# Second layer's attention scores issued together and later, first layer's output projection summed in three parts

## The chip, the cores and the metric

The program runs on one core of one Trainium2 chip. The metric is the device time of one execution in microseconds (us). The kernel before has a median of 2377.14 us over three runs (2376.62 to 2378.21).

## The reference

A trunk of two layers over 256 tokens of 2048 features, in float32. Cut to what matters here:

```python
h = x
for i in range(2):
    hn = rms_norm(h, attn_norm[i])
    mix = windowed_gqa_sink(hn, ...) if i == 0 else diff_attention(hn, ...)   # each ends in  o @ w_o
    h = h + mix
    h = h + swiglu(rms_norm(h, ffn_norm[i]), w_ffn_in[i], w_ffn_out[i])
    gate = sigmoid(rms_norm(h, ple_gate_norm[i]) @ ple_w_gate[i])
    h = h + rms_norm(p[i] @ ple_w_proj[i], ple_post_norm[i]) * gate

# diff_attention, per head (8 heads, two score maps c = 0, 1 each)
probs_c = softmax(q_c @ k_c.T * scale - slope * dist)
o = (probs_0 - lam * probs_1) @ v
```

Layer 0 has 32 query heads in 16 pairs, and each pair gives 128 of the 2048 columns of `o`, so the projection `o @ w_o` sums over 16 blocks of 128 rows of `w_o`.

## The kernel before

**Weights.** All weights stream from HBM as float32 in blocks of 4 x 128 rows by 512 columns (`load_block`, on SP's queue). `split_block` turns two blocks of 128 rows at a time into a high and a low float32r half: ACT casts the high half (L138, tile `ws`), DVE subtracts for the low one (L139). Four `ws` tiles exist, and the split runs up to four ahead (`feed.ahead`). Each product x*w is three matmuls (high x low, low x high, high x high), so one block of 128 rows costs six matmuls of 128x512 (two token halves `m`, three products) at L176, tile `mm`.

**Groups.** A `Group` is one strip of 512 output columns times `n` row blocks: it takes two of the four `mm` PSUM tiles, runs `n` times six matmuls, and calls `done(ps)`. Before row block `k` it calls `flow.until(len(xs) > k)`: if the activation tile `xs[k]` has not been issued yet, all pending side work is issued at once until it has.

**Side work.** Attention, norms and transposes are small pieces that wait in the heap of `Flow`. `flow.later(delay, fn)` puts a piece in; every weight matmul moves the clock of `Flow` on by `MM` = 0.23 and runs one step of the piece that is due, up to its next `yield`. So a `yield` after each small matmul puts one weight matmul between any two of them. The order on PE is exactly the order of issue; ACT, DVE and POOL are ordered by the tile scheduler, which knows their dependences.

**First layer.** `AttentionA`: 16 pairs of heads, each with scores (L410, 128x512), softmax (`exps`, tile `e`), eight transposes of `e` (`keys_first`, L441, tile `wT`), twelve matmuls with the values (`weigh`, L546, 128x256), and a split into `os[j]` (L206 on ACT and L207 on DVE, tile `xt`). `project(w, os, norm)` is the output projection: in two halves of 8 row blocks, four strips each, so that the first half needs only `os[0]` to `os[7]`. Each group's `done` adds its two PSUM tiles to the residual `h` on DVE (`add_to_h`, L298), and in the second half also starts the next norm of that strip (`norm.add`: squares on ACT at L242, then after a delay of 3.0 eight transposes at L269 and their splits at L210 and L211).

**Second layer.** `AttentionB`: four strips of 512 columns, each with a group for the queries, one for the keys and one for the values, of 16 row blocks each; a strip holds two heads. `turn_side` transposes a head's queries or keys (four matmuls at L402, tile `qk`, split at L210 on ACT and L211 on DVE) and, for the keys, queues the two score maps with delays 4.5 and 6.5. `scores` (L410, here 128x256, six matmuls per map) is followed by `exps` and, after the second map, by the mix of the two maps (`r2l`, a scaling on POOL at L610, DVE at L612), then transposes (L441), values (`weigh`, L635) and the transposes of the result (L658). The second layer's projection uses the same `project`.

The program emits, at the end, `groups = attn_a.groups() + project(...) + FeedForward(0) + attn.groups() + project(...) + FeedForward(1)` and runs them one after the other.

Of the kernel before, what the change touches and what calls it, by code (L numbers as in the profile page):

```python
# [18 lines left out]
P = 128  # L19
# [66 lines left out]
def encoder(ctx: ExitStack, tc: tile.TileContext, x, p, attn_norm, ffn_norm, a_w_qkv, a_q_norm,  # L86
# [189 lines left out]
    class Slots:  # L276
# [5 lines left out]
        def __len__(self):  # L282
            n = 0
            while n in self.got:
                n += 1
            return n
# [118 lines left out]

    def scores(ps, q, k):

        for m in range(NM):
            for i, (a, b) in enumerate(((0, 1), (1, 0), (0, 0))):
                nc.tensor.matmul(ps[m], q[:, a, mslice(m)], k[:, b], start=(i == 0), stop=(i == 2))  # L410
                yield

# [146 lines left out]
    class AttentionB:  # L559
# [18 lines left out]
        def turn_side(self, hd, which, toks, b):  # L578
            s = self.hd.setdefault(hd, {"e": {}})
            t = self.ap.tile([P, 2, 2, T], F32R, name=f"qk{which}", tag=f"qk{which}", bufs=2)  # L580
            yield from to_pairs(t, toks, b * T, (gq_b, gk_b)[which])
            s[which] = t
            if which == 1:
                for c in range(2):
                    flow.later(4.5 + 2.0 * c, lambda c=c: self.scores(hd, c))

# [11 lines left out]
        def scores(self, hd, c):  # L598
# [3 lines left out]
            pss = [ps[:, m, :] for m in range(NM)]  # L602
            yield from scores(pss, s[0][:, c], s[1][:, c])
            s["e"][c] = exps(pss, self.dist, 2.0 ** (-8.0 * (hd + 1) / B_H), self.ap)
# [68 lines left out]

    def project(w, os, norm):

        def done(half, s):
            def add(ps):
                add_to_h(ps, s)
                if half == 1:
                    norm.add(s, 3.0)  # L680
            return add
        n = KT // 2

        class Half:
            def __len__(self):
                return max(0, len(os) - n)

            def __getitem__(self, k):
                return os[n + k]
        return [Group(w, half * n * P, n, s, (os, Half())[half], done(half, s))  # L690
                for half in range(2) for s in range(NS)]

# [120 lines left out]
    norm = Norm(C_FFN)  # L813
    groups = attn_a.groups() + project(a_w_o[0], attn_a.os, norm)
    norm_b = Norm(C_ATTN + KT)
    groups += FeedForward(0, norm).groups(norm_b)
    attn = AttentionB(norm_b)
    norm = Norm(C_FFN + KT)
    groups += attn.groups() + project(b_w_o[0], attn.os, norm)
    groups += FeedForward(1, norm).groups(None)  # L820
# [87 lines left out]
```

## Time and profile before

| what | value |
|---|---|
| median of 3 runs | 2377.14 us (2376.62 to 2378.21) |
| the profiled execution's own time | 2379.22 us |
| its span, first to last instruction | 2377.4 us |
| PE busy | 2347.2 us, 99% of the span |
| DVE busy | 1352.4 us, 57% |
| ACT busy | 1121.4 us, 47% |
| mean granted clock of TensorE | 0.997 of full speed |
| share of PE in the chain that ended last | 87% (L176 alone 84%) |

PE is the matmul side of TensorE, PEld its weight loads. The time of a PE row runs to the modelled end of its last matmul; successive matmuls overlap, so the distance from one start to the next is what a matmul costs in a stream. "Idle before" is the time in which an engine did nothing just before the instruction, with the engine that released it.

### The profile page before, as it was taken

What the parts mean: (1) busy time and instruction counts of PE and PEld (TensorE: products, weight loads), DVE (VectorE), ACT (ScalarE), POOL (GpSimd) and SP (SyncE); (2) the same over time, 40 slices, a digit from 0 to 9 for tenths busy, and PEclk for the clock granted to TensorE, in tenths of its full rate; (3) what the DMA queues carried; (4) which work ended last, traced back from release to release, by engine and by line L of the source; (5) the groups of instructions that cost most, each with busy time, mean ns of one, the idle gap of its engine ahead of it and who ended that gap; (6) DMA issues with size and microseconds to landing.
All of it is one profiled execution on the core that took longest, in us unless ns stands there. A gap on an engine that the chain in (4) does not pass through costs nothing.

```text
span 2377.4 us, 28287 instructions
## 1 busy us (share of the span) xinstructions
PE 2347.2 (99%) x10757; PEld 1928.4 (81%) x10757; DVE 1352.4 (57%) x1604; ACT 1121.4 (47%) x1557; POOL 141.4 (6%) x311
## 2 busy tenths in 40 slices
PE   8999999999999999999999999999999999999999
PEld 6877788888888888888878888888888888888887
DVE  5777555555555454566567667655545554455564
ACT  5555454434434434455555554544444434444453
POOL 1342000000000000000110120000000000000000
PEclk9999999999999999999999999999999999999999
DMA  6433455555555555555544545555555555555554
GB/s 236 158 108 106 137 182 191 195 192 189 192 185 190 195 191 191 185 179 193 181 160 162 175 160 179 190 185 185 195 186 195 194 193 183 192 195 195 177 196 141
DMA packets 121569, 428.71 MB, mean 180 GB/s; under 512 B 13552, under 2 KB 16728, under 8 KB 121176
## 3 DMA queue, kind: packets, MB, share of 16 engines
q1 hardware_dynamic: 121432, 426.89, 51.8%
q8 instruction: 84, 1.38, 0.2%
q14 instruction: 53, 0.43, 0.1%
HBM read 424.74 MB, written 2.10 MB: 180 GB/s over the span
## 4 chain that ended last, share of the span: by engine, by line
PE 87%; DVE 1%; ACT 1%; issue 0%; POOL 0%; DVEq 0%; POOLq 0%; ACTq 0%
PE mm L176 84%; PE at L751 1%; PE at L269 1%; PE at L410 1%; PE at L635 1%; DVE ws L139 0%; ACT e L427 0%; PE at L402 0%; DVE e L612 0%; ACT v L210 0%; PE at L441 0%; ACT ws L138 0%; PE at L658 0%; DVE qk L211 0%; POOL e L610 0%
## 5 line engine op out<-in xcount | busy, mean ns | idle before, releaser
L176 PE MATMUL mm<-ws,xt 128*128 128x512 f32 x9600 | 2315.6, 396 | 6.1 <-ACT xt L206 3.9
L176 PEld LDWEIGHTS mm<-ws,xt 128*128 128x128 f32 x9600 | 1792.1, 188 | 404.9 <-ACT xt L206 4.9
L139 DVE TENSOR_TENSOR ws<-raw,ws 128x1024 fp32r<-128x1024 f32 x800 | 978.0, 1224 | 874.2 <-ACT ws L138 873.5
L138 ACT CAST ws<-raw 128x1024 fp32r<-128x1024 f32 x800 | 840.8, 1052 | 1026.8 <-PE mm L176 957.2
L217 POOL TENSOR_SCALAR rs_v<-ssum 128x2 f32<-128x2 f32 x8 | 1.5, 193 | 1707.5 <-DVE ssum L246 1707.5
L298 DVE TENSOR_TENSOR h<-mm,h 128x512 f32<-128x512 f32 x96 | 62.2, 682 | 2.3 <-PE mm L176 2.2
L210 ACT ACTIVATE xt<-at,gains 128x256 fp32r<-128x256 f32 x96 | 44.1, 474 | 32.9 <-DVE xt L211 24.2
L269 PE MATMUL at<-ident,h 128*128 128x128 f32 x192 | 52.4, 287 | 6.2 <-DMA h<-in_x_dram 6.2
L427 ACT ACTIVATE e<-e,nm 128x257 f32<-128x257 f32 (+1 forms) x96 | 48.0, 503 | 21.1 <-DVE nm L424 20.7
L206 ACT CAST xt<-at 128x256 fp32r<-128x256 f32 x108 | 37.9, 372 | 39.9 <-DVE xt L207 31.8
L211 DVE SCALAR_TENSOR_TENSOR xt<-at,gains,xt 128x256 fp32r<-128x256 f32 x96 | 44.7, 480 | 17.8 <-ACT xt L210 17.8
L207 DVE TENSOR_TENSOR xt<-at,xt 128x256 fp32r<-128x256 f32 x108 | 43.3, 418 | 14.0 <-ACT xt L206 14.0
L219 POOL TENSOR_TENSOR rs_y<-rs_v,halves 128x2 f32<-128x2 f32 (+2 forms) x29 | 49.0, 1691 | 2.4
L751 PE MATMUL at<-ident,hid 128*128 128x128 f32 x176 | 47.8, 272 | 0.0
L546 PE MATMUL at<-wT,vp 128*128 128x256 f32 x192 | 45.7, 297 | 1.3 <-DVE wT L207 1.0
L421 DVE SCALAR_TENSOR_TENSOR e<-dist,at 128x256 f32<-128x256 f32 x96 | 36.4, 413 | 10.2 <-PE at L410 9.8
L441 PE MATMUL at<-ident,e 128*128 128x128 f32 x160 | 40.6, 272 | 0.7 <-DVE e L421 0.7
L410 PE MATMUL at<-kd,qT 128*128 128x512 f32 x96 | 36.1, 400 | 3.2 <-DVE wT L207 2.5
L732 ACT ACTIVATE silu<-mm,rinv 128x512 f32<-128x512 f32 x44 | 29.9, 688 | 19.7 <-PE mm L176 19.7
L526 POOL TENSOR_SCALAR e<-e,rd 128x256 f32<-128x256 f32 x64 | 33.0, 532 | 60.4 <-DVE rd L430 60.0
L546 PEld LDWEIGHTS at<-wT,vp 128*128 128x128 f32 x192 | 33.9, 204 | 2.9 <-ACT e L427 1.1
L269 PEld LDWEIGHTS at<-ident,h 128*128 128x128 f32 x192 | 27.7, 147 | 9.4 <-DMA h<-in_x_dram 7.1
(97 smaller groups left out, 671.7 us busy)
## 6 DMA issues: line engine op xcount, KB each, us to landing
raw<-in_w_ffn_in_dram SPq DMA_DIRECT2D x352, 512.0 KB
raw<-in_w_ffn_out_dram SPq DMA_DIRECT2D x176, 512.0 KB
raw<-in_b_w_qkv_dram SPq DMA_DIRECT2D x96, 512.0 KB
raw<-in_ple_w_gate_dram SPq DMA_DIRECT2D x64, 512.0 KB
raw<-in_a_w_qkv_dram SPq DMA_DIRECT2D x40, 512.0 KB
raw<-in_a_w_o_dram SPq DMA_DIRECT2D x32, 512.0 KB
raw<-in_b_w_o_dram SPq DMA_DIRECT2D x32, 512.0 KB
raw<-in_ple_w_proj_dram SPq DMA_DIRECT2D x16, 256.0 KB
```

Source lines behind the costliest of these rows:

```text
L138: nc.scalar.copy(out=ws[:, 0], in_=src)
L139: nc.vector.tensor_tensor(out=ws[:, 1], in0=src, in1=ws[:, 0].bitcast(F32), op=ALU.subtract)
L176: nc.tensor.matmul(ps[m], x[:, a, mslice(m)], w, start=(k == 0 and i == 0), stop=(k == self.n - 1 and i == 2))
L210: nc.scalar.activation(out=hi, in_=src, func=AF.Copy, scale=scale)
L211: nc.vector.scalar_tensor_tensor(out=lo, in0=src, scalar=scale, in1=hi.bitcast(F32), op0=ALU.mult, op1=ALU.subtract)
L219: nc.gpsimd.tensor_tensor(out=y, in0=v, in1=halves[:, :n], op=ALU.pow)
L269: nc.tensor.transpose(ps[:, j, mslice(m)], h[:, m, (k + j) * P:(k + j + 1) * P], ident)
L298: nc.vector.tensor_tensor(out=hs, in0=ps[m], in1=hs, op=ALU.add)
L410: nc.tensor.matmul(ps[m], q[:, a, mslice(m)], k[:, b], start=(i == 0), stop=(i == 2))
L427: nc.scalar.activation(out=sc[:, m, :], in_=sc[:, m, :], func=AF.Exp, bias=nm[:, m:m + 1], accum_out=den[:, m:m + 1])
L546: nc.tensor.matmul(ps, v[:, a, c0:c0 + P], wT[:, b, kh, :], start=(n == 0), stop=(n == 11))
L751: nc.tensor.transpose(ps[:, j, mslice(m)], hid[m][:, (j0 + j) * P:(j0 + j + 1) * P], ident)
```

## The change

Three edits. `scores` gets an argument `together`: the second layer's six score matmuls of a map are issued in one piece, without a weight matmul between them, and then move the flow's clock by 0.7 once. The two score maps of a second-layer head are queued with delays 6.5 and 8.5 in place of 4.5 and 6.5. `project` takes the sizes of its parts: the first layer's projection runs in parts of 8, 4 and 4 row blocks, the second layer's in 8 and 8 as before; the norm is started by the last part.

```diff
--- before.py
+++ after.py
@@ -403,12 +403,15 @@
                 yield
         split_scaled(dst[:, :, 0, :], dst[:, :, 1, :], ps, g)
 
-    def scores(ps, q, k):
+    def scores(ps, q, k, together=False):
 
         for m in range(NM):
             for i, (a, b) in enumerate(((0, 1), (1, 0), (0, 0))):
                 nc.tensor.matmul(ps[m], q[:, a, mslice(m)], k[:, b], start=(i == 0), stop=(i == 2))
-                yield
+                if not together:
+                    yield
+        if together:
+            yield 0.7
 
     def exps(pss, d, slope, ap, extra=None):
 
@@ -582,7 +585,7 @@
             s[which] = t
             if which == 1:
                 for c in range(2):
-                    flow.later(4.5 + 2.0 * c, lambda c=c: self.scores(hd, c))
+                    flow.later(6.5 + 2.0 * c, lambda c=c: self.scores(hd, c))
 
         def values(self, s):
             def done(ps):
@@ -600,7 +603,7 @@
             flow.until(lambda: 0 in s and 1 in s) if not (0 in s and 1 in s) else None
             ps = at_ps()
             pss = [ps[:, m, :] for m in range(NM)]
-            yield from scores(pss, s[0][:, c], s[1][:, c])
+            yield from scores(pss, s[0][:, c], s[1][:, c], True)
             s["e"][c] = exps(pss, self.dist, 2.0 ** (-8.0 * (hd + 1) / B_H), self.ap)
             if c == 1:
                 (e1, r1), (e2, r2) = s["e"][0], s["e"][1]
@@ -671,24 +674,29 @@
             return out
 
 
-    def project(w, os, norm):
-
-        def done(half, s):
+    def project(w, os, norm, parts):
+
+        class Part:
+            def __init__(self, first):
+                self.first = first
+
+            def __len__(self):
+                return max(0, len(os) - self.first)
+
+            def __getitem__(self, k):
+                return os[self.first + k]
+
+        def done(last, s):
             def add(ps):
                 add_to_h(ps, s)
-                if half == 1:
+                if last:
                     norm.add(s, 3.0)
             return add
-        n = KT // 2
-
-        class Half:
-            def __len__(self):
-                return max(0, len(os) - n)
-
-            def __getitem__(self, k):
-                return os[n + k]
-        return [Group(w, half * n * P, n, s, (os, Half())[half], done(half, s))
-                for half in range(2) for s in range(NS)]
+        out, first = [], 0
+        for n in parts:
+            out += [Group(w, first * P, n, s, Part(first), done(first + n == KT, s)) for s in range(NS)]
+            first += n
+        return out
 
     class FeedForward:
         def __init__(self, layer, norm):
@@ -811,12 +819,12 @@
 
     attn_a = AttentionA(norm_a)
     norm = Norm(C_FFN)
-    groups = attn_a.groups() + project(a_w_o[0], attn_a.os, norm)
+    groups = attn_a.groups() + project(a_w_o[0], attn_a.os, norm, (8, 4, 4))
     norm_b = Norm(C_ATTN + KT)
     groups += FeedForward(0, norm).groups(norm_b)
     attn = AttentionB(norm_b)
     norm = Norm(C_FFN + KT)
-    groups += attn.groups() + project(b_w_o[0], attn.os, norm)
+    groups += attn.groups() + project(b_w_o[0], attn.os, norm, (8, 8))
     groups += FeedForward(1, norm).groups(None)
     feed = Feed(groups)
 
```

PE at the end of the first layer's attention (`e` the softmax weights, `wT` their transposes, `vp` the values, `mm` the projection, `h` the residual being transposed for the next norm). Before:

```order
L441 MATMUL at<-ident,e 128x128 x4
L546 MATMUL at<-wT,vp_433 128x256 x3
L546 MATMUL at<-wT,vp_437 128x256 x3
...
L176 MATMUL mm<-ws,xt 128x512 x11
...
L176 MATMUL mm<-ws,xt 128x512 x6
L441 MATMUL at<-ident,e 128x128 x8
...
L176 MATMUL mm<-ws,xt 128x512 x20
L269 MATMUL at<-ident,h 128x128
```

Now (L444 and L549 are the lines 441 and 546 of before):

```order
L444 MATMUL at<-ident,e 128x128
L176 MATMUL mm<-ws,xt 128x512 x2
L549 MATMUL at<-wT,vp_433 128x256
L176 MATMUL mm<-ws,xt 128x512
...
L444 MATMUL at<-ident,e 128x128
L176 MATMUL mm<-ws,xt 128x512 x17
L549 MATMUL at<-wT,vp_433 128x256
L176 MATMUL mm<-ws,xt 128x512
...
L549 MATMUL at<-wT,vp_437 128x256
L176 MATMUL mm<-ws,xt 128x512 x44
L269 MATMUL at<-ident,h 128x128
```

The runs of attention matmuls without a weight matmul between them are gone: every transpose and value matmul of the last three head pairs now has one beside it, there are 17 between the last transposes and the last values, and 44 between the last values and the first transpose of the norm.

PE at the first strip of the second layer, from the last key transpose of the strip's first head to the first transposes of `e` (`qk` the split queries and keys, `qn` the normed keys before they are transposed). Before:

```order
L176 MATMUL mm<-ws,xt 128x512 x21
L410 MATMUL at<-qk_9066,qk_8893 128x256
L176 MATMUL mm<-ws,xt 128x512
L410 MATMUL at<-qk_9066,qk_8893 128x256
...
L176 MATMUL mm<-ws,xt 128x512 x2
L402 MATMUL at<-ident,qn 128x128
...
L176 MATMUL mm<-ws,xt 128x512 x21
L410 MATMUL at<-qk_9164,qk_8946 128x256
```

Now:

```order
L176 MATMUL mm<-ws,xt 128x512 x30
L410 MATMUL at<-qk_9082,qk_8909 128x256 x6
L176 MATMUL mm<-ws,xt 128x512 x2
L402 MATMUL at<-ident,qn 128x128
...
L176 MATMUL mm<-ws,xt 128x512 x2
L410 MATMUL at<-qk_9082,qk_8909 128x256 x6
L176 MATMUL mm<-ws,xt 128x512 x25
L410 MATMUL at<-qk_9154,qk_8962 128x256 x6
L176 MATMUL mm<-ws,xt 128x512 x5
L410 MATMUL at<-qk_9154,qk_8962 128x256 x6
L176 MATMUL mm<-ws,xt 128x512 x5
L444 MATMUL at<-ident,e 128x128
```

The first head's second map now comes after the second head's key transposes, and between those transposes and the second head's scores there are 27 weight matmuls and six score matmuls where there were 21 weight matmuls.

DVE in the same strip (`v` the split values, `nm` the row maxima, `rd` and `r2l` the softmax factors). Before:

```order
L421 SCALAR_TENSOR_TENSOR e<-dist,at 128x256 x2
L211 SCALAR_TENSOR_TENSOR v_9169<-mm,rinv,v_9169 128x256
L424 TENSOR_REDUCE nm<-e 128x2
L430 RECIPROCAL rd<-den 128x2 x2
L608 TENSOR_SCALAR r2l<-rd,nlam 128x2
L211 SCALAR_TENSOR_TENSOR v_9172<-mm,rinv,v_9172 128x256
L612 SCALAR_TENSOR_TENSOR e<-e,rd 128x256 x2
L211 SCALAR_TENSOR_TENSOR v_9175<-mm,rinv,v_9175 128x256
L211 SCALAR_TENSOR_TENSOR v_9178<-mm,rinv,v_9178 128x256
L139 TENSOR_TENSOR ws<-raw,ws 128x1024
L211 SCALAR_TENSOR_TENSOR qk_9164<-at,cols,qk_9164 128x2x256
```

Now (L424, L427, L433, L611 and L615 are the lines 421, 424, 430, 608 and 612 of before):

```order
L211 SCALAR_TENSOR_TENSOR v_9166<-mm,rinv,v_9166 128x256
L211 SCALAR_TENSOR_TENSOR qk_9154<-at,cols,qk_9154 128x2x256
L424 SCALAR_TENSOR_TENSOR e<-dist,at 128x256 x2
L427 TENSOR_REDUCE nm<-e 128x2
L433 RECIPROCAL rd<-den 128x2
L211 SCALAR_TENSOR_TENSOR v_9169<-mm,rinv,v_9169 128x256
L211 SCALAR_TENSOR_TENSOR v_9172<-mm,rinv,v_9172 128x256
L139 TENSOR_TENSOR ws<-raw,ws 128x1024
L211 SCALAR_TENSOR_TENSOR v_9175<-mm,rinv,v_9175 128x256
L433 RECIPROCAL rd<-den 128x2
L611 TENSOR_SCALAR r2l<-rd,nlam 128x2
L615 SCALAR_TENSOR_TENSOR e<-e,rd 128x256 x2
```

The split of the second head's keys moved from behind the mix of the first head's maps, all four value splits and a weight split to the place behind the first value split; the mix now stands behind all four value splits and one weight split.

## Rows read from the trace of the kernel before

**Rows 1.** The page's first part, busy time by engine.

```profile
PE 2347.2 (99%) x10757; PEld 1928.4 (81%) x10757; DVE 1352.4 (57%) x1604; ACT 1121.4 (47%) x1557; POOL 141.4 (6%) x311
```

**Rows 2.** Windows: stretch, length, each engine's busy (count), granted clock, DMA share, GB/s.

```profile
250.00:260.00 10.00, 7.38 (x24) 5.81 (x24) 2.74 (x5) 2.54 (x4) 0.94 (x2) 0.66 0.66 234
1218.00:1222.00 4.00, 4.00 (x16) 3.38 (x15) 2.57 (x4) 1.32 (x4) 0.00 (x0) 0.57 0.81 285
```

**Rows 3.** PE by line and shape, 247.80 to 271.42 us, with idle time before.

```profile
L176 PE MATMUL mm<-ws,xt 128*128 128x512 f32 x38 | 12.8, 479 | 4.2 <-ACT xt L206 2.9 <-DVE xt L207 1.2
L546 PE MATMUL at<-wT,vp 128*128 128x256 f32 x36 | 5.9, 306 | 0.6 <-DVE wT L207 0.3 <-ACT wT L206 0.3
L441 PE MATMUL at<-ident,e 128*128 128x128 f32 x11 | 1.5, 272 | 0.0
```

**Rows 4.** Timeline of PE around that stretch: start, duration, what, idle before.

```profile
247.50 0.60 PE L441 MATMUL at<-ident,e 128*128 128x128 f32 x4
247.86 1.68 PE L546 MATMUL at<-wT,vp 128*128 128x256 f32 x12
...
271.43 0.27 PE L269 MATMUL at<-ident,h 128*128 128x128 f32 x1
```

**Rows 5.** The chain that ended last, one run of weight matmuls: start, us, what.

```profile
317.29 12.74 PE mm L176 x56
```

**Rows 6.** Timeline of PE, first layer: eight transposes and twelve value matmuls, interleaved.

```profile
194.99 0.27 PE L441 MATMUL at<-ident,e 128*128 128x128 f32 x1
...
197.39 0.27 PE L441 MATMUL at<-ident,e 128*128 128x128 f32 x1
...
209.52 0.28 PE L546 MATMUL at<-wT,vp 128*128 128x256 f32 x1
...
213.33 0.28 PE L546 MATMUL at<-wT,vp 128*128 128x256 f32 x1
```

**Rows 7.** Waits of PE, 1195 to 1460 us: us in total, times, longest.

```profile
PE at L410 <- DVE qk L211: 5.0, 4, 2.3
```

**Rows 8.** Timeline of PE, second layer, strips one and two: around the wait.

```profile
1209.43 5.04 PE L176 MATMUL mm<-ws,xt 128*128 128x512 f32 x21
1216.73 0.39 PE L410 MATMUL at<-qk,qk 128*128 128x256 f32 x1 [2.27 <-DVE qk L211]
...
1223.07 0.27 PE L441 MATMUL at<-ident,e 128*128 128x128 f32 x1
...
1288.97 5.04 PE L176 MATMUL mm<-ws,xt 128*128 128x512 f32 x21
1294.91 0.38 PE L410 MATMUL at<-qk,qk 128*128 128x256 f32 x1 [0.91 <-DVE qk L211]
...
1299.70 0.27 PE L441 MATMUL at<-ident,e 128*128 128x128 f32 x1
```

**Rows 9.** PEld by line, 1195 to 1460 us: the weight loads of the scores.

```profile
L410 PEld LDWEIGHTS at<-qk,qk 128*128 128x128 f32 x96 | 18.7, 195 | 7.2 <-DVE qk L211 6.7
```

**Rows 10.** Timeline, first strip: first head's last score, then the mix on DVE.

```profile
1207.78 0.28 PE L410 MATMUL at<-qk,qk 128*128 128x256 f32 x1
...
1213.00 1.10 DVE L612 SCALAR_TENSOR_TENSOR e<-e,rd 128x256 f32<-128x256 f32 x2 [0.28 <-POOL e L610]
```

**Rows 11.** Timeline of DVE, first strip: a value split, a weight split, the key split.

```profile
1208.98 0.48 DVE L211 SCALAR_TENSOR_TENSOR v<-mm,rinv,v 128x256 fp32r<-128x256 f32 x1
...
1214.81 1.21 DVE L139 TENSOR_TENSOR ws<-raw,ws 128x1024 fp32r<-128x1024 f32 x1
1215.94 0.73 DVE L211 SCALAR_TENSOR_TENSOR qk<-at,cols,qk 128x512 fp32r<-128x512 f32 x1
```

**Rows 12.** DVE by line, 268 to 316 us: four long groups of the second half.

```profile
L139 DVE TENSOR_TENSOR ws<-raw,ws 128x1024 fp32r<-128x1024 f32 x16 | 19.6, 1225 | 14.1 <-ACT ws L138 14.1
L211 DVE SCALAR_TENSOR_TENSOR xt<-at,gains,xt 128x256 fp32r<-128x256 f32 x16 | 7.5, 481 | 2.2 <-ACT xt L210 2.2
L298 DVE TENSOR_TENSOR h<-mm,h 128x512 f32<-128x512 f32 x8 | 5.2, 684 | 0.8 <-PE mm L176 0.8
```

## The prediction, made before the changed kernel was run

> **What bounds the kernel now.** I read the busy times first: PE is busy for 99% of the span, every other engine for 57% or less [rows 1]. So only two things can shorten the time: less work on PE, or the stretches in which PE waits or runs at a lower clock. The change adds and removes no matmul, so all of it must come from the second kind. The next view was the windows, read for a granted clock below 1. Besides the start of the program two places stand out, and the change touches both: 250 to 260 us, at the end of the first layer's attention, with a granted clock of 0.66 and PE busy for 7.38 of 10 us, and 1218 to 1222 us, in the first strip of the second layer's attention, with 0.57 [rows 2]. A mean between 0.5 and 1 is a mixture of the two levels, 1.2 and 2.4 GHz; in both cases the fall comes right behind a wait of PE. The reader is to see in these rows that a wait here costs more than its own length.
>
> The PE rows of the first place name its waits: from 247.80 to 271.42 us PE sits idle for 4.2 us before weight matmuls, for the splits of the attention's output on ACT and DVE, and 0.6 us before value matmuls [rows 3]. The timeline shows why: four transposes and then twelve value matmuls in one run, with no weight matmul beside them [rows 4]. The projection has come to a row block whose activation was not yet issued, so all pending side work is issued at once, and PE then has nothing to do until it has gone through ACT and DVE. In the second layer the view of waits has a single entry: 5.0 us in four waits, the longest 2.3, of the scores for the key split on DVE [rows 7].
>
> **The price of a matmul in a stream.** A weight matmul takes 12.74 / 56 = 0.2275 us [rows 5]. Interleaved with weight matmuls, seven steps from transpose to transpose take 2.40 us, 0.343 each, so a transpose costs 0.343 - 0.2275 = 0.115 us; eleven steps between value matmuls take 3.81 us, 0.346 each, so a 128x256 matmul costs 0.119 us [rows 6].
>
> **Part one: the projection in three parts.** With parts of 8, 4 and 4, the four groups of the middle part (96 weight matmuls) need only `os[8]` to `os[11]`, and the last head pairs find weight matmuls to run beside. The order of the instructions shows that no run of side work is left there, and that 44 weight matmuls lie between the last values and the norm's first transpose. What this frees: from 247.50 to 271.43 us are 23.93 us [rows 4]. In them lie 38 weight matmuls, 36 value matmuls and twelve transposes (eleven in the row, and the first at 247.50) [rows 3, 4]. At the stream's prices they take 38 x 0.2275 + 36 x 0.119 + 12 x 0.115 = 8.65 + 4.28 + 1.38 = 14.3 us. **Gain 9.6 us.** As a check from the other side: 4.8 us of waits [rows 3] and 0.34 x 10 = 3.4 us of lost clock [rows 2] make 8.2; the remaining 1.4 us is the draining of PE at each wait, which the trace counts as busy (a matmul's row lasts 0.28 us where the next could start after 0.12).
>
> The earlier runs of side work in the first half of this projection stay as they are, since the first part is still 8. What is added is eight residual additions on DVE, of 5.2 / 8 = 0.65 us each [rows 12]. I cost them at nothing: in the last part a group now takes 24 x 0.2275 + 8 x 0.115 = 6.4 us of PE, and DVE has in it two weight splits, four norm splits and two additions, 2 x 1.225 + 4 x 0.47 + 2 x 0.65 = 5.6 us [rows 12]. That leaves 0.75 us per group, the thinnest cover of the whole forecast; if it goes, the next group but one waits for its PSUM tiles (a rival below). The DMA issues are the same 4-block pieces in another order, one for every 24 weight matmuls as everywhere; no step is moved past SP's queue.
>
> **Part two: later scores.** In each strip the second head's scores wait for the key split. In strip one, from 1209.43 to 1223.07 us, are 13.64 us with 35 weight matmuls (21 ahead of the scores, 14 between and behind them) and twelve scores: 7.96 + 1.43 = 9.4 us at the stream's prices, so 4.25 us are lost. In strip two it is 10.73 us for the same work: 1.34 us lost [rows 8]. The remaining two waits share 5.0 - 2.27 - 0.91 = 1.8 us [rows 7, 8], so I take them like strip two. Together 4.25 + 3 x 1.34 = 8.3 us, of which 5.0 are the waits, 0.43 x 4 = 1.7 the clock in strip one [rows 2], and the rest draining and restarting.
>
> The change gives that split 27 weight matmuls and six scores of head start in place of 21 weight matmuls, some 2.1 us more, against a longest wait of 2.27. More than that, DVE's order changes: the key split stood behind the mix of the first head's maps (which waits for POOL), the value splits and a weight split; it now stands right behind the first value split. It should be ready by about the time that the first value split is done, some 5 us before PE asks for it. **Gain 8.3 us.** What is late next is the mix itself: from the first head's last score to its first transpose there are now 35 weight matmuls and twelve scores, 9.5 us, and the chain between them took from 1207.78 to 1214.10, 6.3 us [rows 10], with up to three value splits and a weight split newly ahead of it on DVE, 3 x 0.48 + 1.21 = 2.65 us [rows 11]. That makes 9.0 us at most on DVE, and I take it as hidden, by half a microsecond.
>
> **Part three: scores without a weight matmul between them.** No row shows 128x256 scores back to back. The nearest row is the run of twelve value matmuls, of the same shape and with a new weight load each: (1.68 - 0.28) / 11 = 0.127 us [rows 4], against 0.119 interleaved. So 96 scores cost 96 x 0.008 = **0.8 us more**; I take this value because shape, loads and accumulation are the same. The lower bound is that they stream better than interleaved ones, which I put at the same 0.8 us as a gain. The upper bound is that the weight loads set the pace: a score's load takes 0.195 us [rows 9], so 96 x (0.195 - 0.119) = 7.3 us. A rule speaks against this part: the Trainium skill, page "TensorE: Matmul & The Clock Gate", section "Part 3: Packing small matmuls", says that a weight load overlaps running matmuls only where it goes to other rows of the array. By that rule every score's load would stand in the open; the run of twelve at 0.127 us each, less than one load, speaks against it here.
>
> **Sum.** 9.6 + 8.3 - 0.8 = 17.1 us. The profiled execution took 2379.22 us itself, 1.8 us around its span of 2377.4, and would take 2362.1. It lies 2.1 us above the median of the runs; against the median of 2377.14 us I forecast **2360.0 us**. Differences under 0.2%, 4.75 us, count as no change: about what a measurement of this kernel can tell from none.
>
> **Rivals.**
>
> *The wait moves to the mix.* If the three value splits and the weight split are late on ACT as well as on DVE, the first head's transposes wait: 6.3 + 2 x 2.65 = 11.6 us against 9.5, 2.1 us in each of four strips, 8.4 us. For it: half a microsecond of cover. Against it: one value split already stood in the old chain, and ACT and DVE work on successive tiles at the same time. Time 2368.4 us, still faster. Chance 0.07.
>
> *The loads of the scores come into the open.* As a pace: 17.9 - 7.3 = 10.6 us gained, 2366.5 us; chance 0.04. One after another, load and then stream: each score costs 0.195 us more, 18.7 us in all [rows 9], which eats the gain of 17.9: 2377.9 us, no change. The Trainium skill's rule on weight loads above would give this second case. Chance 0.01, because of the run at 0.127 us.
>
> *The short groups become bound by DVE*, the rival on the other side. In the four long groups of before, DVE sat idle for 14.1 + 2.2 + 0.8 = 17.1 us in front of this work, 4.3 us per group [rows 12]. If a short group keeps these waits, because its additions, norm splits and weight splits wait for each other, it takes 5.6 + 4.3 = 9.9 us in place of 6.4. In the last part alone that is 4 x 3.5 = 14 us, and the time comes to 2374, no change: 0.02. If the middle part, which has the attention's end in place of the norm, pays the same, it is 28 us, and the time is 2388, slower: 0.03. It decides from 17.1 / 8 = 2.1 us of excess per short group on, that is 2.9 us of idle time kept. Against it: 14.1 of the 17.1 us are waits for ACT's weight cast, which runs up to four tiles ahead of PE; such a wait is slack and shrinks when DVE is late. Also, DVE's order puts each addition between the norm splits of the strip before, so that two groups overlap.
>
> That the change does not do what it says is ruled out by the order on PE.
>
> **How the numbers follow.** The forecast has 0.83. Its own range runs from 2357.5 (scores streaming better by 0.8 us twice over, and about 1 us of spread between runs) to 2364 (4 us of small new waits in the crowded stretches). The rivals add 0.07 and 0.04 up to 2368.4, and 0.01, 0.02 and 0.03 above. The range to 2368.5 takes in the pace bound of the loads and the wait at the mix, and leaves out the rest and the forecast's own tails. Faster: 0.83 + 0.07 + 0.04 = 0.94. No change: 0.01 + 0.02 = 0.03. Slower: 0.03.
>
> **What would show it.** Right: no wait of PE on ACT or DVE between 248 and 270 us, granted clock 1.0 there and around 1215 us; PE's waits for `qk` gone; scores 0.127 us apart; PE's busy time down while its matmul count stays 10757. Wrong: waits of L176 on DVE's `h` or `ws` in the short groups (the third rival), of the transposes of `e` on the mix (the first), or scores 0.19 us apart and more (the second). The forecast falls if the first layer's projection still shows idle PE in its middle and last part, or if the time lies above 2368.5 us.

## The result, and the profile after

The changed kernel has a median of 2360.83 us over four runs (2359.83 to 2360.86), against 2377.24 us (2376.62 to 2378.21) for the kernel before on the same chip: a ratio of 0.993, with a 95% interval of 0.9912 to 0.9947. The forecast was 2360.0 us, in a range of 2357.5 to 2368.5.

The first part of the profile after answers to [rows 1]. PE's busy time fell from 2347.2 to 2339.4 us with the same 10757 matmuls, though less than the span did.

```profile
PE 2339.4 (99%) x10757; PEld 1925.4 (82%) x10757; DVE 1356.5 (58%) x1612; ACT 1120.2 (47%) x1557; POOL 140.5 (6%) x311
```

The windows of the two places of [rows 2] in the profile after (columns as there; in the second the same work now stands some ten microseconds earlier): PE is busy without a gap, and the granted clock is 1.00 in both.

```profile
250.00:260.00 10.00, 10.00 (x58) 8.44 (x57) 6.18 (x11) 4.76 (x8) 0.93 (x2) 1.00 0.49 161
1200.00:1210.00 10.00, 10.00 (x53) 8.41 (x52) 8.39 (x16) 7.32 (x16) 0.94 (x2) 1.00 0.34 109
```

The end of the first layer's attention, PE's timeline after, answers to [rows 4]. The last values and the norm's first transpose now lie 44 weight matmuls apart, and no row carries an idle time.

```profile
259.36 4.12 PE L176 MATMUL mm<-ws,xt 128*128 128x512 f32 x17
...
267.25 10.17 PE L176 MATMUL mm<-ws,xt 128*128 128x512 f32 x44
277.26 0.27 PE L269 MATMUL at<-ident,h 128*128 128x128 f32 x1
```

PE by line and shape from 245.0 to 277.2 us, after, answers to [rows 3]. All three kinds of work have an idle time of 0.0 where two of them had 4.2 and 0.6.

```profile
L176 PE MATMUL mm<-ws,xt 128*128 128x512 f32 x116 | 32.8, 403 | 0.0
L549 PE MATMUL at<-wT,vp 128*128 128x256 f32 x36 | 10.1, 280 | 0.0
L444 PE MATMUL at<-ident,e 128*128 128x128 f32 x16 | 4.3, 272 | 0.0
```

The waits of PE over the whole span, after (us in total, times, longest). The entry of [rows 7] for `qk` is gone, and nothing has taken its place in the second layer. What is left are waits of the start and of the middle of the first layer.

```profile
PE at L269 <- DMA h<-in_x_dram: 5.2, 2, 3.9
PE at L410 <- DVE wT L207: 2.5, 1, 2.5
...
PE mm L176 <- ACT xt L206: 0.9, 2, 0.5
...
PE at L549 <- DVE wT L207: 0.7, 1, 0.7
```

Strip one of the second layer on PE, after, answers to [rows 8]: no row carries a wait, and the second head's scores stand in two runs of six.

```profile
1198.77 5.83 PE L176 MATMUL mm<-ws,xt 128*128 128x512 f32 x25
1204.44 0.87 PE L410 MATMUL at<-qk,qk 128*128 128x256 f32 x6
1205.15 1.32 PE L176 MATMUL mm<-ws,xt 128*128 128x512 f32 x5
1206.31 0.88 PE L410 MATMUL at<-qk,qk 128*128 128x256 f32 x6
1207.02 1.32 PE L176 MATMUL mm<-ws,xt 128*128 128x512 f32 x5
1208.18 0.27 PE L444 MATMUL at<-ident,e 128*128 128x128 f32 x1
```

**Where the time went.** Two marks are the same in every kernel here: the first transposes of the first layer's queries (`qn`, L402) and the first transposes of `p` after its projection. The stage between them is called the first-layer stage below. It took 239.4 us before (76.6 to 316.0) and 229.8 after (75.7 to 305.5): 9.6 us less. From the second mark to the end of the span it was 2061.4 us, and is 2053.6: 7.8 us less. Ahead of the first mark are 0.9 us, where the load of `x` landed earlier in this execution (PE's wait for it 5.2 us in place of 6.2); the change has no part in that. Together 18.3 us, the difference of the two spans; without the start it is 17.4, against the 17.1 us of the forecast.

### The profile page after: what moved, and what is told of

Its sections match the earlier page's. It is cut to its first block, busy times and chain, and to the rows that moved or that the text cites. A ratio compares the mean times of both kernels' runs of the same rounds, so it can differ in the third digit from the quotient of the medians.

```text
span 2359.1 us, 28290 instructions
## 1 busy us (share of the span) xinstructions
PE 2339.4 (99%) x10757; PEld 1925.4 (82%) x10757; DVE 1356.5 (58%) x1612; ACT 1120.2 (47%) x1557; POOL 140.5 (6%) x311
## 4 chain that ended last, share of the span: by engine, by line
PE 97%; DVE 1%; DMA 1%; ACT 0%; POOL 0%; issue 0%; SPq 0%; DVEq 0%; ACTq 0%
PE mm L176 92%; PE at L410 1%; PE at L549 1%; PE at L759 1%; PE at L269 1%; PE at L444 1%; PE at L638 1%; PE at L402 0%; DVE ws L139 0%; DMA raw<-in_a_w_qkv_dram 0%; DMA vec<-in_ffn_norm_dram 0%; ACT ws L138 0%; POOL rs_y L219 0%; DVE e L424 0%; PE at L661 0%
## 5 line engine op out<-in xcount | busy, mean ns | idle before, releaser
L298 DVE TENSOR_TENSOR h<-mm,h 128x512 f32<-128x512 f32 x104 | 67.8, 684 | 2.6 <-PE mm L176 2.3
L211 DVE SCALAR_TENSOR_TENSOR xt<-at,gains,xt 128x256 fp32r<-128x256 f32 x96 | 44.7, 480 | 16.3 <-ACT xt L210 16.3
L549 PE MATMUL at<-wT,vp 128*128 128x256 f32 x192 | 49.2, 286 | 0.7 <-DVE wT L207 0.7
L444 PE MATMUL at<-ident,e 128*128 128x128 f32 x160 | 42.2, 272 | 0.7 <-DVE e L424 0.7
L424 DVE SCALAR_TENSOR_TENSOR e<-dist,at 128x256 f32<-128x256 f32 x96 | 36.2, 412 | 2.5 <-PE at L410 2.5
L549 PEld LDWEIGHTS at<-wT,vp 128*128 128x128 f32 x192 | 34.7, 194 | 1.8 <-ACT e L430 1.1
```

The costliest lines, as they stand in the source:

```text
L211: nc.vector.scalar_tensor_tensor(out=lo, in0=src, scalar=scale, in1=hi.bitcast(F32), op0=ALU.mult, op1=ALU.subtract)
L298: nc.vector.tensor_tensor(out=hs, in0=ps[m], in1=hs, op=ALU.add)
L444: nc.tensor.transpose(ps[:, kh, mslice(m)], w[:, m, kh * P:(kh + 1) * P], ident)
L549: nc.tensor.matmul(ps, v[:, a, c0:c0 + P], wT[:, b, kh, :], start=(n == 0), stop=(n == 11))
```

## The experiments

Twelve further runs were made, on four chips. The table gives each one's median, the median of the kernel before on the same chip, the 95% interval of the ratio of the two, and the first-layer stage and the rest of the span from its profile. "Waits for `qk`" are PE's in the second layer.

| run | median us (lowest to highest) | before | ratio, 95% interval | first-layer stage | rest | waits for `qk` |
|---|---|---|---|---|---|---|
| before | | | | 239.4 | 2061.4 | 5.0 |
| the change | 2360.83 (2359.83 to 2360.86) | 2377.24 | 0.9912 to 0.9947 | 229.8 | 2053.6 | none |
| e1 parts only | 2368.61 (2365.97 to 2369.39) | 2376.03 | 0.9952 to 0.9977 | 228.7 | 2059.6 | 5.0 |
| e2 scores only | 2369.91 (2366.82 to 2370.69) | 2376.03 | 0.9958 to 0.9982 | 239.4 | 2053.6 | none |
| e3 delay only | 2368.85 (2366.23 to 2369.15) | 2376.03 | 0.9951 to 0.9976 | 239.6 | 2052.9 | none |
| e4 together only | 2369.74 (2367.20 to 2370.81) | 2376.03 | 0.9959 to 0.9982 | 239.6 | 2053.7 | none |
| e5 dose on DVE | 2367.35 (2366.38 to 2368.05) | 2378.58 | 0.9939 to 0.9969 | 234.8 | 2054.3 | none |
| e6 parts 4, 4, 4, 4 | 2367.45 (2366.63 to 2367.80) | 2378.58 | 0.9939 to 0.9972 | 236.0 | 2053.9 | none |
| e7 parts 6, 4, 2, 2, 2 | 2360.01 (2359.17 to 2360.88) | 2378.58 | 0.9909 to 0.9938 | 228.4 | 2054.2 | none |
| e8 parts 4, then six of 2 | 2366.31 (2366.08 to 2366.70) | 2378.58 | 0.9935 to 0.9965 | 234.6 | 2054.2 | none |
| e9 the change again | 2361.35 (2361.02 to 2361.93) | 2375.18 | 0.9928 to 0.9956 | 230.1 | 2053.5 | none |
| e10 as e7, again | 2358.67 (2357.25 to 2359.50) | 2375.18 | 0.9917 to 0.9942 | 227.3 | 2054.1 | none |
| e11 parts 8, 2, 2, 2, 2 | 2361.29 (2358.81 to 2362.41) | 2377.01 | 0.9918 to 0.9945 | 230.6 | 2054.2 | none |
| e12 parts 6, 2, 4, 4 | 2359.78 (2358.99 to 2360.42) | 2377.01 | 0.9914 to 0.9941 | 227.9 | 2053.8 | none |

### Each part alone

**e1, the parts of the projection alone.** The change with the second layer's edits undone:

```diff
-                    flow.later(6.5 + 2.0 * c, lambda c=c: self.scores(hd, c))
+                    flow.later(4.5 + 2.0 * c, lambda c=c: self.scores(hd, c))
...
-            yield from scores(pss, s[0][:, c], s[1][:, c], True)
+            yield from scores(pss, s[0][:, c], s[1][:, c])
```

> Only the first layer's projection in parts of 8, 4 and 4; the second layer's scores as before. Theory (each part of the gain is the removal of its own waits, with the clock and the draining that hang on them): 9.6 us less than before, so a ratio of 0.9960 and about 2367.6 us; the second layer keeps its four waits of 5.0 us in total for the key split. Rival (the gain of the first layer is partly given back by the eight added residual additions, and the whole gain of the change came from the second layer): under 5 us less.

It is 7.4 us faster than the kernel before by the medians, and its first-layer stage is 228.7 us: this part stands alone. (It is 1.1 us shorter than the change's. The granted clock from 160 to 190 us is 1.00 in e1 and 0.94 in the change, which is enough to make that difference; that place is shown under e11 and e12.) The waits for `qk` are back, and they are those of [rows 7] in number and length:

```profile
PE at L410 <- DVE qk L211: 5.0, 4, 2.3
```

What is not back is the fall of the clock. PE's timeline of strip one in e1, with the same 21 weight matmuls and the same wait as in [rows 8], and below it the window behind the wait:

```profile
1197.99 5.04 PE L176 MATMUL mm<-ws,xt 128*128 128x512 f32 x21
1205.29 0.39 PE L410 MATMUL at<-qk,qk 128*128 128x256 f32 x1 [2.26 <-DVE qk L211]
...
1210.02 0.27 PE L444 MATMUL at<-ident,e 128*128 128x128 f32 x1
```

```profile
1206.00:1210.00 4.00, 4.00 (x24) 3.44 (x23) 3.18 (x6) 1.33 (x2) 0.00 (x0) 1.00 0.79 272
```

The stretch takes 1210.02 - 1197.99 = 12.03 us where it took 13.64 before, 1.6 us less, with a granted clock of 1.00 where [rows 2] show 0.57. The wait was equal (2.26 and 2.27 us); its price was not.

**e2, the second layer's edits alone.** The change with the first layer's projection in two parts:

```diff
-    groups = attn_a.groups() + project(a_w_o[0], attn_a.os, norm, (8, 4, 4))
+    groups = attn_a.groups() + project(a_w_o[0], attn_a.os, norm, (8, 8))
```

> Only the scores together and 2.0 later; the first layer's projection in two halves as before. Theory: 8.1 us less than before, ratio 0.9966, about 2369.1 us, and the two single parts add up to the whole change. Rival (the parts share a cause, such as weight tiles that run further ahead): the two gains add up to clearly more or less than the 16.4 us of the whole.

6.1 us faster by the medians. The first-layer stage is that of before to 0.1 us, and the rest is that of the change to 0.1 us. In the traces the parts are independent: each has its gain in its own stage, whether or not the other is there.

**e3, the delays alone.** As e2, and without `together`:

```diff
-            yield from scores(pss, s[0][:, c], s[1][:, c], True)
+            yield from scores(pss, s[0][:, c], s[1][:, c])
```

> The scores 2.0 later, but each still with a weight matmul beside it; projection as before. Theory (what counts is the place of the key split in DVE's queue and the head start, not that the scores run together; back to back they take 0.118 us each against 0.119 interleaved): the four waits for the key split go, 8 us less than before, about 2369 us, the same as scores only. Rival (running the scores together is what frees time): under 3 us less.

**e4, the scores together alone.** As e2, with the old delays:

```diff
-                    flow.later(6.5 + 2.0 * c, lambda c=c: self.scores(hd, c))
+                    flow.later(4.5 + 2.0 * c, lambda c=c: self.scores(hd, c))
```

> The scores together, with the old delays 4.5 and 6.5; projection as before. DVE's order here has the key split behind the softmax of the first head but ahead of its mix, with 21 weight matmuls of head start as before. Theory of the queue's place: the waits go here too, 6 to 8 us less than before, 2369 to 2371 us. Rival (the head start of two more microseconds is what removes the wait): waits of about 4 us in total stay, under 4 us less.

Either edit alone takes all four waits away: the rest of the span is 2052.9 us in e3 and 2053.7 in e4, against 2053.6 with both. They do the same thing twice. In e4 PE has the same 21 weight matmuls ahead of the scores as before, and yet the scores don't wait. DVE's timeline of e4 tells why (first the key split, then the mix, with the second softmax factor and a value split between them; below it PE's):

```profile
1207.75 0.75 DVE L211 SCALAR_TENSOR_TENSOR qk<-at,cols,qk 128x512 fp32r<-128x512 f32 x1 [0.30 <-ACT qk L210]
...
1209.85 1.09 DVE L615 SCALAR_TENSOR_TENSOR e<-e,rd 128x256 f32<-128x256 f32 x2 [0.28 <-POOL e L613]
```

```profile
1206.41 5.04 PE L176 MATMUL mm<-ws,xt 128*128 128x512 f32 x21
1211.28 0.87 PE L410 MATMUL at<-qk,qk 128*128 128x256 f32 x6
```

The split ends at 1208.50, 2.8 us before PE asks for it, and the mix comes behind it. Before, the mix started at 1213.00 and the split at 1215.94 behind it [rows 10, 11]. So the earlier place of the split in DVE's order is enough, with no more weight matmuls in front of the scores than before. Whether more weight matmuls alone, with DVE's order of before, would have been enough was not run.

### The cover on DVE

**e5, a dose of work on DVE in the last part's groups.** Six sums along the rows of `h` are added to each group of the first layer's last part, ahead of its norm; their results are used nowhere:

```diff
                 if last:
+                    for _ in range(6 if len(parts) == 3 else 0):
+                        nc.vector.reduce_sum(out=small("dose", 1, 1), in_=h[:, 0, s * W:(s + 1) * W], axis=AX.X)
                     norm.add(s, 3.0)
```

> The changed kernel with six reductions of 128x512 on DVE, about 0.6 us each, added behind the residual additions of each of the four short groups of the last part; their results are not used. That makes DVE's work in such a group about 5.6 + 3.7 = 9.3 us against 6.4 us of PE. Theory (DVE may fall behind there, because weight tiles are split up to four ahead, about 8 us of PE's work, and it catches up in the next layer part): the 4 x 2.9 = 12 us of excess are mostly absorbed, 0 to 5 us slower than the change, 2361 to 2366 us. Rival (the short groups are paced by DVE, and the cover of 0.75 us was all there is): 12 us slower or more, 2373 us.

The last part's stretch in the change, DVE by line from 275 to 301 us, answers to [rows 12] (busy, mean ns, then idle time):

```profile
L139 DVE TENSOR_TENSOR ws<-raw,ws 128x1024 fp32r<-128x1024 f32 x8 | 9.8, 1225 | 4.9 <-ACT ws L138 4.9
L211 DVE SCALAR_TENSOR_TENSOR xt<-at,gains,xt 128x256 fp32r<-128x256 f32 x15 | 6.9, 478 | 0.5 <-ACT xt L210 0.5
L298 DVE TENSOR_TENSOR h<-mm,h 128x512 f32<-128x512 f32 x7 | 4.8, 686 | 0.1
```

DVE's idle time has come down from 17.1 us in four long groups to 5.5 us in four short ones, 4.3 to about 1.4 each, while PE's is nil: it was slack. With the dose the view of waits and the lines of DVE (275 to 303 us) read:

```profile
PE at L269 <- DVE h L298: 4.6, 2, 2.3
```

```profile
L694 DVE TENSOR_REDUCE dose<-h 128x1 f32<-128x512 f32 x19 | 12.9, 678 | 0.0
L139 DVE TENSOR_TENSOR ws<-raw,ws 128x1024 fp32r<-128x1024 f32 x7 | 8.5, 1218 | 0.0
```

DVE's idle time is gone, PE waits twice for an addition, and the stage is 5.0 us longer than the change's. The dose is 6 x 0.678 = 4.1 us per group, 16.3 in all, of which some 11 stayed hidden. The median, 2367.35 us, lies some 6 us above those of the change (on other chips): a little more than the theory's 0 to 5, and half of the rival's 12. So the bound that the prediction's third rival named does exist; the change stays clear of it.

### Other divisions of the projection

**e6, four parts of 4.**

```diff
-    groups = attn_a.groups() + project(a_w_o[0], attn_a.os, norm, (8, 4, 4))
+    groups = attn_a.groups() + project(a_w_o[0], attn_a.os, norm, (4, 4, 4, 4))
```

> The changed kernel with the first layer's projection in four parts of 4. By the order on PE the two long runs of side work in the first half, of 34 and 38 attention matmuls without a weight matmul beside them, become four runs of 11, 4, 32 and 12. In the changed kernel the two runs lose 5.5 and 3.0 us against the stream's prices. Theory (the runs cost by the waits that they leave): 3 to 5 us faster than the change, 2356 to 2358 us. Rival (eight more short groups, sixteen more additions than before in all, make DVE the limit there): no gain or slower than the change.

**e7, parts of 6, 4, 2, 2 and 2.** The weights of this projection are packed for the parts on the host, so that they come in 16 pieces of 512 KB and 32 of 256 KB in place of 32 of 512 KB (in e8, e11 and e12 too some pieces are of 256 KB):

```diff
-    groups = attn_a.groups() + project(a_w_o[0], attn_a.os, norm, (8, 4, 4))
+    groups = attn_a.groups() + project(a_w_o[0], attn_a.os, norm, (6,4,2,2,2))
...
-    for n in ('a_w_qkv', 'a_w_o', 'b_w_qkv', 'b_w_o', 'w_ffn_in', 'ple_w_proj', 'ple_w_gate'):
+    given["a_w_o"] = _strips(given["a_w_o"], (6,4,2,2,2))
+    for n in ('a_w_qkv', 'b_w_qkv', 'b_w_o', 'w_ffn_in', 'ple_w_proj', 'ple_w_gate'):
```

> The changed kernel with the first layer's projection in parts of 6, 4, 2, 2 and 2. By the order on PE the first long run of 34 stays and the second of 38 is gone. Theory: about 3 us faster than the change, 2358 us. Rival (DVE the limit): no gain or slower.

**e8, a part of 4 and six of 2.** As e7, with these numbers:

```diff
-    groups = attn_a.groups() + project(a_w_o[0], attn_a.os, norm, (8, 4, 4))
+    groups = attn_a.groups() + project(a_w_o[0], attn_a.os, norm, (4,2,2,2,2,2,2))
```

> The changed kernel with the first layer's projection in parts of 4 and six times 2: by the order on PE only a run of 13 and one of 6 stay. DVE gets 32 residual additions more than in the change, about 21 us. Theory: 5 to 8 us faster than the change, 2353 to 2356 us, since DVE has room around it. Rival (DVE or the PSUM tiles of groups of only 12 weight matmuls become the limit): the gain is eaten, with waits of weight matmuls on the additions or on weight tiles.

e6 and e8 went the way of their rivals: a first part of 4 costs some 5 to 6 us of stage against the change, with either of the two divisions that follow it. e7 is within 1 us of the change's first median, on another chip. PE's timeline of e8 shows the largest single wait, and DVE's of the same stretch what stands in front of it:

```profile
166.05 0.80 PE L176 MATMUL mm<-ws,xt 128*128 128x512 f32 x1 [3.37 <-DVE h L298]
```

```profile
160.33 0.69 DVE L391 TENSOR_TENSOR qn<-mm,rr 128x512 f32<-128x512 f32 x1 [2.76 <-POOL rr L379]
160.94 1.22 DVE L139 TENSOR_TENSOR ws<-raw,ws 128x1024 fp32r<-128x1024 f32 x1
162.07 1.08 DVE L424 SCALAR_TENSOR_TENSOR e<-dist,at 128x256 f32<-128x256 f32 x3
...
165.32 1.27 DVE L298 TENSOR_TENSOR h<-mm,h 128x512 f32<-128x512 f32 x2
```

A short group wants PSUM tiles that an addition must free, and the addition stands on DVE behind a norm's product that waits 2.76 us for POOL, a weight split and eight more instructions of the attention (row maxima, softmax factors and a query split among them). e6 has the same wait of 3.4 us. Here, in the crowded middle of the attention, is where the additions of short groups are late on DVE; at the end, where the prediction put its rival, PE waits for no addition in any of these divisions. The wait of 3.4 us is not the whole price, though: it stands in place of a wait of 2.5 us that the other divisions have there (below), and PE's waits of weight matmuls for the splits of the attention's output come to 4.9 us in e6 and 4.5 in e8, against 1.1 in the change.

**e9 and e10, the change and e7 again on one chip,** with no further edit.

> The changed kernel itself, on the same chip as the next run and as its own runs of before. Theory: 16 to 18 us less than before, ratio 0.993. The first layer's stage and the second layer's stage of its trace should repeat within the loss of clock that the waits at 163 to 186 us may or may not bring: about 1.5 us.

> Parts of 6, 4, 2, 2 and 2 again, beside the change on the same chip. Theory: the second long run of side work is gone (3 us by the stream's prices) and twelve groups of 12 weight matmuls add work on DVE that stays hidden, so 1 to 3 us faster than the change. Rival: equal within 1 us, the lost run having only moved its waits.

Parts of 6, 4, 2, 2 and 2 are 2.7 us faster than the change by the medians, and the two ranges of runs (2357.25 to 2359.50, 2361.02 to 2361.93) don't touch. It is the fastest version of this study.

**e11 and e12, which end of the division does it.** As e7, with these numbers:

```diff
-    groups = attn_a.groups() + project(a_w_o[0], attn_a.os, norm, (8, 4, 4))
+    groups = attn_a.groups() + project(a_w_o[0], attn_a.os, norm, (8,2,2,2,2))
```

```diff
-    groups = attn_a.groups() + project(a_w_o[0], attn_a.os, norm, (8, 4, 4))
+    groups = attn_a.groups() + project(a_w_o[0], attn_a.os, norm, (6,2,4,4))
```

> The first layer's projection in parts of 8, 2, 2, 2 and 2 row blocks, all else as the change. Question: which end of the division 6, 4, 2, 2, 2 made it 2.7 us faster than the change. By the order of the instructions the change issues two runs of 34 and 38 attention matmuls without a weight matmul beside them in the first part; 8, 2, 2, 2, 2 keeps both, 6, 4, 2, 2, 2 has only the one of 34. Theory A, the shorter first part does it, by the run of 38, which at the stream's prices loses 3.0 us: this kernel is as fast as the change, first-layer stage (first query transposes to first transposes of p) 229.5 to 230.5 us against 229.8 and 230.1, and slower than 6, 2, 4, 4 on the same chip by 1.5 to 3 us. Theory B, the short parts at the end do it: stage 227.5 to 228.5 us, faster than 6, 2, 4, 4 by 1.5 to 3 us. Theory C, the last groups of 12 weight matmuls become bound by DVE (two norm additions and a weight split in 3.65 us of PE): stage 233 us or more, with waits of L176 on DVE h.

> The first layer's projection in parts of 6, 2, 4 and 4 row blocks, all else as the change: the first part of 6, 4, 2, 2, 2 and the last part of the change. By the order of the instructions it has the run of 34 attention matmuls and none of 38, and a new short one of 9. Theory A, the shorter first part makes the gain of 2.7 us: stage 227.5 to 229 us, and 1.5 to 3 us faster than 8, 2, 2, 2, 2 on the same chip. Theory B, the short parts at the end make it: stage 229.5 to 230.5 us, as the change, and slower than 8, 2, 2, 2, 2.

e12 is 1.5 us faster than e11 by the medians, at the lower end of what theory A asked for, and the two ranges overlap. Its stage is 227.9 us, e11's 230.6. That looks like theory A, but the granted clocks below undo it. What is shown is that short groups at the end cost nothing, against theory C: in e11 DVE is busy for 23.07 of 27.00 us in the last part, and PE never waits (window from 275 to 302 us; the second number is PE's, the fourth DVE's).

```profile
275.00:302.00 27.00, 27.00 (x135) 21.70 (x134) 23.07 (x37) 18.10 (x38) 2.73 (x6) 1.00 0.69 235
```

The distance between the two stages is the clock again. Every kernel here but e6 and e8 has, in the middle of the first layer's attention, the same wait of 2.5 us of a score for a transposed weight, with 24 value matmuls in one run behind it. PE's timeline there in e12, in the change and in e11:

```profile
168.96 0.93 PE L410 MATMUL at<-kd,qT 128*128 128x512 f32 x3 [2.50 <-DVE wT L207]
169.72 3.01 PE L549 MATMUL at<-wT,vp 128*128 128x256 f32 x24
```

```profile
168.55 1.62 PE L410 MATMUL at<-kd,qT 128*128 128x512 f32 x3 [2.50 <-DVE wT L207]
169.97 3.74 PE L549 MATMUL at<-wT,vp 128*128 128x256 f32 x24
```

```profile
168.62 1.62 PE L410 MATMUL at<-kd,qT 128*128 128x512 f32 x3 [2.51 <-DVE wT L207]
170.04 5.03 PE L549 MATMUL at<-wT,vp 128*128 128x256 f32 x24
```

The same 24 matmuls take 3.01, 3.74 and 5.03 us. The window from 160 to 190 us around them shows granted clocks of 1.00, 0.94 and 0.89, in the same order:

```profile
160.00:190.00 30.00, 26.34 (x141) 20.68 (x139) 24.82 (x47) 17.33 (x41) 10.52 (x24) 1.00 0.25 82
```

```profile
160.00:190.00 30.00, 24.59 (x128) 19.05 (x128) 24.77 (x53) 17.72 (x48) 10.86 (x25) 0.94 0.12 41
```

```profile
160.00:190.00 30.00, 24.59 (x121) 19.24 (x120) 23.89 (x51) 16.80 (x48) 10.20 (x24) 0.89 0.12 43
```

In this run of values alone e11 lost 5.03 - 3.01 = 2.0 us against e12, and in the three scores ahead of it another 0.7 (1.62 against 0.93), behind the same wait: that is as much as the 2.7 us between their stages. As an estimate, take off each stage what its clock lost in this window, 30 us times what is missing to 1.00. It takes off a little too much, since some of the loss falls into the wait. Then 227.9 us are left for e12, 230.6 - 3.3 = 227.3 for e11, and 228.0 to 228.7 for the three executions of 8, 4, 4 (the change, e9 and e1); for 6, 4, 2, 2, 2, with clocks of 0.89 in e7 and 0.94 in e10, it is 225.1 and 225.5. So e11 and e12 don't differ by more than this estimate can tell, and neither comes near e7 and e10: neither theory A nor theory B alone accounts for their gain. That gain is not the clock's, since e10 and the change had the same 0.94 there; which feature of 6, 4, 2, 2, 2 makes it stays open.

## Why the prediction was right, point by point

**The bound.** That nothing but PE's waits and their clock could be gained held: the matmul count is unchanged, and the waits and falls of both places are gone.

**Part one** was forecast at 9.6 us and measured 9.6 (239.4 to 229.8). Taking the whole stretch between two marks and subtracting its matmuls at the price of the stream counted waits, clock and draining at once; the sum of waits and lost clock alone, 8.2 us, would have been short. That the two agree to a tenth is partly luck: the three executions of 8, 4, 4 have stages of 228.7 to 230.1 us, as the clock fell or not behind the wait of 2.5 us. The cover of 0.75 us on DVE held, for the reason given: the idle time in front of the weight splits was slack.

**Part two with part three** was forecast at 8.3 - 0.8 = 7.5 us and measured 7.8. The total came out, partly by luck, and three of its steps did not hold as put:

- *The cost of scores without a weight matmul between them*, 0.8 us, was mis-sized. In the change they follow each other in (1205.15 - 1204.44) / 6 = 0.118 us, which is the 0.119 us of the interleaved ones. The row that set the price, twelve value matmuls at 0.127 us each [rows 4], did not carry over: the 24 values of e12 take (3.01 - 0.28) / 23 = 0.119. In before, eleven more at 264.46 us (1.57 us long) give 0.129, so the twelve were no single slow run; why both were slower stays open. The second rival falls with it: the loads of the scores, in the profile after (shortest, median and longest in ns), take about as long as in [rows 9], and yet they are hidden behind matmuls that start 0.118 us apart. The rule named there (the Trainium skill, page "TensorE: Matmul & The Clock Gate", section "Part 3: Packing small matmuls", that a weight load overlaps running matmuls only where it goes to other rows) does not agree with these rows; the same section also lets a load into a background weight buffer go ahead, which does.

```profile
L410 PEld LDWEIGHTS at<-qk,qk x96: 187/189/193, 1195.1 to 1432.8; 128*128 128x128 f32 x96
```

- *The head start*, 27 weight matmuls and six scores in place of 21 weight matmuls, was not needed (e4). Of the two reasons that the prediction gave, the second, DVE's order, was enough. In the change the split is done at 1198.52 + 0.75 = 1199.27 and asked for at 1204.44, 5.2 us later; the forecast was some 5.
- *The clock's 1.7 us in strip one* is no fixed part of the price. It stood in the profiled execution of before, and not in that of e1, with the same wait. Against e1, which kept its clock there, these edits are worth 2059.6 - 2053.6 = 6.0 us and not 7.8; that the total came near the forecast needed an execution of before that had lost it.

The mix kept more of its cover than the half microsecond of the forecast. From the profile after, DVE in strip one:

```profile
1198.52 0.75 DVE L211 SCALAR_TENSOR_TENSOR qk<-at,cols,qk 128x512 fp32r<-128x512 f32 x1 [0.31 <-ACT qk L210]
...
1205.23 1.09 DVE L615 SCALAR_TENSOR_TENSOR e<-e,rd 128x256 f32<-128x256 f32 x2 [0.69 <-POOL e L613]
```

It ends at 1206.32, and PE asks for it at 1208.18: 1.9 us to spare, so the first rival did not happen.

**From the trace to the medians.** The two single parts add up to 7.4 + 6.1 = 13.5 us by their medians, while the forecast was 17.1 and the first comparison gave 16.4. The runs tell why they differ. Each run has its mean granted clock. Of the 36 runs of the kernel before in the experiments, the 18 with 0.996 or 0.997 took 2377.1 to 2379.3 us, the five with 0.998 took 2375.2 to 2377.0, and the 13 with 0.999 or 1.000 took 2372.9 to 2375.2. The profiled execution of before had 0.997, and the forecast was made against it. All nine runs of the change had 0.999 and took 2359.8 to 2361.9. So the change is worth some 13 us against an execution of before that kept its clock, and some 17 against one that did not; 13.8 us in e9 lie between. That the first comparison had runs of before of 2376.6 to 2378.2 us, close to the profiled one, was luck for the forecast of 17.1. This is a correlation over runs with one clock figure each; only the profiled executions show where the clock fell.

## What to carry to other kernels

Price a stall as a whole stretch between two marks less its matmuls at the rate of the stream: waits, draining and clock are then counted together, and once. Before giving a late operand more head start, look at its place in the order of the engine that makes it: moving the split ahead of the mix, which waits for other engines (e4), was worth as much as moving the consumer as well. When a reduction is cut into shorter groups, look at what stands ahead of the instruction that frees their PSUM tile: cut where that engine has no waits for others in its queue. Here a first part of 4 row blocks cost 5 to 6 us, and parts of 4 and of 2 at the end cost nothing. And before two versions with 2 or 3 us between them are ranked, compare their granted clocks.

## What the hardware showed that was not expected

A wait of one and the same length has no one price. Behind a wait of 2.26 to 2.27 us in strip one the granted clock was 0.57 in one execution and 1.00 in another; behind a wait of 2.50 to 2.51 us in the first layer the same 24 matmuls took 3.01, 3.74 or 5.03 us; and the two waits of 2.3 us in e5 left it at 1.00 (275 to 303 us). The Trainium skill, page "TensorE: Matmul & The Clock Gate", section "What's actually happening", says that the gate looks at activity in a window that runs free of the kernel, so that the same kernel differs from run to run; the runs agree with it in that, though none here shows the window itself.
